# A GLA head's score matmuls issued in one burst, in turn over the array's column groups, and new lengths for fp32 matmuls in the planner

## The chip, the cores and the metric

One core of a Trainium2 chip. TensorE (PE) multiplies: it loads a stationary operand and streams the columns of a moving operand past it into PSUM. ScalarE (ACT) and VectorE (DVE) do element-wise work, GpSimd (POOL) a little, SyncE (SP) issues most DMAs. The metric is the device time of one execution in microseconds. Before the change it is 2159.78 us, the median of three runs (2157.18 to 2162.58).

## The reference

Two layers on 256 tokens of width 2048, everything in fp32. Layer 0 mixes tokens by native sparse attention (NSA), layer 1 by gated linear attention (GLA); each layer ends in a squared-ReLU MLP of width 8192. The part that matters here is the GLA mixer, 4 heads of key width 256 and value width 512:

```
h = rms_norm(x); q, k, v, g, r = split(h @ w_in)
log_a = log_sigmoid(g @ w_gate_up + b_gate) / 16
for each chunk of 64 tokens:
    cum   = cumsum(log_a)
    decay = exp(cum_i - cum_j) for j <= i
    att   = einsum(q_i, k_j, decay_ij)
    o     = (q * exp(cum)) @ state + att @ v
    state = exp(last) * state + (k * exp(last - cum)).T @ v
o = rms_norm(o) * silu(r);  x = x + o @ w_out
```

The kernel doesn't go chunk by chunk. For each head it makes the whole lower triangle of 256 x 256 scores with their decays, and multiplies it by the values.

## The kernel before, in words

The weights are fp32 and stream in by DMA. Each block of 128 x 1024 is split into a rounded part (ACT, the cast `wh`) and the rest (DVE, `wl`), and PE multiplies in three terms: high by high, high by low, low by high. These wide matmuls (`psa<-wh,op` and `psa<-wl,op`, 512 columns) fill nearly all of PE's time.

The mixers' own work is written as Python generators ("streams") that are stepped between the wide matmuls. The class `Plan` decides when: `mm` and the other helpers add an estimated cost to a clock for each engine (`W.run`), a stream yields the planned time from which its next piece is ready (`W.ready`) and the PSUM banks it needs (`{"aux": 1}`), and `W.tick`, called after every three wide matmuls, steps the streams whose time has come. So the order on each engine is fixed when the program is built, by the planner's costs. An fp32 matmul that isn't marked fp32r was counted as `max(4 * n / 2.4 + 3, 214)` ns (n moving columns).

The function `attn` (L1607 on) makes one head's scores. First the decays: products with the 0/1 matrix `cum`, exponentials on ACT, times keys and queries on DVE, into two tiles `e[0]` and `e[1]` (the head's 256 keys in two halves, `cc`; in the trace all these tiles are named `g`). Then the score matmuls by level: level 0 joins the two token blocks of 128, level 1 the halves of 64 within a block, level 2 those of 32, and levels 3 to 7 go down to single tokens. All are fp32, accumulated over `cc`:

- level 0: 2 matmuls, 128 stationary columns by 128 moving ones, into the bank `pc`;
- level 1: 4 of 64 by 64 and level 2: 8 of 32 by 32, into the bank `pa`, all of level 1 into partitions 0 to 63;
- levels 3 to 7: ten blocks (level, token block) of four matmuls, 32 by 64, into the bank `pq`; block i goes to partitions 32*(i%4), that is to one of the array's four groups of 32 columns.

The trace has every such fp32 matmul as two passes (two LDWEIGHTS and two MATMULs). In the old code the four matmuls of a block, eight passes, follow each other into the same column group:

```
for i, (l, t) in enumerate(blocks):
    for h in range(2):
        for cc in range(2):
            mm(pq[32 * (i % 4):32 * (i % 4) + 32, i // 4, own[h]], ...)
    if i % 4 == 3:
        yield 0.0
```

The yields part a head's 54 score matmuls into five bursts (2; 12; 16; 16; 8 matmuls) with three or six wide matmuls between them. Behind each bank ACT copies: `pc` and `pa` into `att` (one copy of 128 x 128, then six small ones), `pq` into the head of `e[0]`. Then PE transposes that (`psx<-cid,g`), DVE merges it into `att` with 20 predicated copies (L1715), ACT and DVE split `att` into `ath`, and `head_out` multiplies by the values (`psx<-g,ath`).

Of the kernel before, what the change touches and what calls it, by code (L numbers as in the profile page):

```python
# [18 lines left out]
P = 128  # L19
T = 256  # L20
NT = 2
# [102 lines left out]
def trunk_kernel(ctx: ExitStack, tc: tile.TileContext, a: dict, out: bass.AP):  # L124
# [3 lines left out]
    W = Plan()  # L128
    uid = [0]

    def nm(s):
        uid[0] += 1
        return f"{s}_{uid[0]}"
# [15 lines left out]
    def free(ap):  # L149
        n = 1  # L150
        for d in ap.shape[1:]:
            n *= d
        return n

    def in_psum(ap):
        return W.key(ap).startswith("ps")

    def mm(dst, lhsT, rhs, **kw):
        n = free(rhs)
        if lhsT.dtype == F32R:  # L160
            c = max(n / 2.4 + 13.0, 109.0)
        else:
            c = max(4 * n / 2.4 + 3, 214.0)
        W.run("pe", c, [dst], [lhsT, rhs])
        nc.tensor.matmul(dst, lhsT, rhs, skip_group_check=True, **kw)  # L165

# [27 lines left out]
    def copy(dst, src):  # L194
        W.run("act", free(src) * 0.833 + (60 if in_psum(src) else 100), [dst], [src])
        nc.scalar.copy(dst, src)  # L196

    def tt(dst, x, y, op):
        W.run("dve", free(dst) * 1.042 + 75, [dst], [x, y])
        nc.vector.tensor_tensor(dst, x, y, op=op)  # L200
# [46 lines left out]
    def aux(shape, dtype=F32):  # L247
        t = paux.tile(shape, dtype, tag="aux", name=nm("psx"))
        W.take("aux", t)
        return t  # L250
# [1229 lines left out]
    def gla(prep, after):  # L1480
        op = prep.op
        NLEV = 8
        with tc.tile_pool(name="gla1", bufs=1) as s1, tc.tile_pool(name="gla2", bufs=1) as s2:
# [131 lines left out]
            def attn(hd, kq, dg, wait, res):  # L1615


                while not all(w["done"] for w in wait):
                    yield 0.0
                e = []  # L1620
                for cc in range(2):
                    c = (2 * hd + cc) * P
                    yield W.ready(kq, cum, *las), {"g8": 1}
                    et = g8([P, NLEV, 2, P])
                    for t in range(NT):
                        yield 0.0, {"aux": 1}

                        pe_ = aux([P, 2, P])
                        for h in range(2):
                            mm(pe_.rearrange("p l k -> p (l k)"), las[2 * t + h][:, c:c + P],  # L1630
                               cum[:, 384 * h + t * P:384 * h + t * P + 2 * P], start=(h == 0), stop=(h == 1))
                        act(et[:, 0, t, :], pe_[:, t, :], AF.Exp)
                        act(et[:, 1, :, t * 64:t * 64 + 64], pe_[:, 1 - t, :].rearrange("p (s k) -> p s k", s=2), AF.Exp)
                        W.give(pe_, W.t["act"])
                        for b in (2 * t, 2 * t + 1):
                            yield 0.0, {"aux": 1}
                            pe_ = aux([P, NLEV - 2, 2, 32])
                            mm(pe_.rearrange("p l s k -> p (l s k)"), las[b][:, c:c + P], cum[:, 768:1152],
                               start=True, stop=True)
                            act(et[:, 2:NLEV, :, b * 32:b * 32 + 32], pe_, AF.Exp)  # L1640
                            W.give(pe_, W.t["act"])
                    for l in range(NLEV):
                        if l % 4 == 0:
                            yield W.ready(et)
                        hs = 128 >> l
                        ev = et[:, l, :, :].rearrange("p s (b r) -> p s b r", r=hs)
                        src = kq[:, cc, 0, :]
                        src = bass.AP(tensor=src.tensor, offset=src.offset,
                                      ap=[list(src.ap[0]), [T + hs, 2], [2 * hs, T // (2 * hs)], [1, hs]])
                        tt(ev, ev, src, ALU.mult)  # L1650
                    e.append(et)
                W.give(kq, W.t["dve"])
                att = s1.tile([P, 3, P], F32, name=nm("att")) if not shared else shared[0]
                if not shared:
                    shared.append(att)
                yield W.ready(*e), {"aux": 1}
                pc = aux([P, 512])
                for cc in range(2):
                    mm(pc[:, 0:P], e[cc][:, 0, 0, :], e[cc][:, 0, 1, :], start=(cc == 0), stop=(cc == 1))
                copy(att[:, 2, :], pc[:, 0:P])  # L1660
                W.give(pc, W.t["act"])
                own = [slice(64 * h, 64 * h + 64) for h in range(2)]
                yield 0.0, {"aux": 1}

                pa = aux([P, 512])
                for t in range(NT):
                    for cc in range(2):
                        tok = e[cc][:, 1, :, t * 64:t * 64 + 64]
                        mm(pa[0:64, t * P:t * P + 64], tok[:, 0, :], tok[:, 1, :], start=(cc == 0), stop=(cc == 1))
                    for h in range(2):  # L1670
                        for cc in range(2):
                            tok = e[cc][:, 2, :, t * 64 + 32 * h:t * 64 + 32 * h + 32]
                            mm(pa[64 * h:64 * h + 32, t * P + 64:t * P + 96], tok[:, 0, :], tok[:, 1, :],
                               start=(cc == 0), stop=(cc == 1))
                for t in range(NT):
                    ts(att[:, t, :], ident, dg[:, t:t + 1], None, ALU.mult)
                yield W.ready(pa)
                for t in range(NT):
                    copy(att[0:64, t, 64:128], pa[0:64, t * P:t * P + 64])
                    for h in range(2):  # L1680
                        copy(att[64 * h:64 * h + 32, t, 64 * h + 32:64 * h + 64],
                             pa[64 * h:64 * h + 32, t * P + 64:t * P + 96])
                give(pa)

                yield 0.0, {"aux": 1}
                pq = aux([P, 4, P])
                blocks = [(l, t) for l in range(3, NLEV) for t in range(NT)]
                for i, (l, t) in enumerate(blocks):
                    hs = 128 >> l
                    for h in range(2):  # L1690
                        for cc in range(2):
                            tok = e[cc][:, l, :, t * 64 + 32 * h:t * 64 + 32 * h + 32]
                            mm(pq[32 * (i % 4):32 * (i % 4) + 32, i // 4, own[h]], tok[:, 1, :],
                               tok.rearrange("p s (b r) -> p b s r", r=hs),
                               start=(cc == 0), stop=(cc == 1))
                    if i % 4 == 3:
                        yield 0.0
                W.give(e[1])
                at = e[0].rearrange("p l s k -> p (l s k)")[:, 0:3 * P].rearrange("p (i k) -> p i k", k=P)
                copy(at[:, 0:2, :], pq[:, 0:2, :])  # L1700
                copy(at[0:64, 2, :], pq[0:64, 2, :])
                W.give(pq, W.t["act"])
                yield W.ready(at), {"aux": 1}
                pl = aux([P, 512])
                for i in range(3):
                    n = P if i < 2 else 64
                    transpose(pl[:, i * P:i * P + n], at[0:n, i, :], ident[0:n, 0:n])
                W.give(e[0])
                yield W.ready(pl)
                for i, (l, t) in enumerate(blocks):  # L1710
                    hs = 128 >> l
                    for h in range(2):
                        dst = att[own[h], t, own[h]].rearrange("p (b s r) -> p b s r", s=2, r=hs)[:, :, 1, :]
                        W.run("dve", 110.0, [att], [pl])
                        nc.vector.copy_predicated(  # L1715
                            dst, lmask[own[h], l - 3, :].rearrange("p (b r) -> p b r", r=hs),
                            pl[own[h], 32 * i:32 * i + 32].rearrange("p (b r) -> p b r", r=hs))
                    if i % 4 == 3:
                        yield 0.0
                W.give(pl, W.t["dve"])  # L1720
                yield W.ready(att), {"ath": 1}
                ah = atile([P, 2, 3, P], F32R)
                copy(ah[:, 0, :, :], att)
                yield W.ready(ah)
                tt(ah[:, 1, :, :], att, ah[:, 0, :, :].bitcast(F32), ALU.subtract)
                res.append(ah)
# [261 lines left out]
```

## Time and profile before

| | before |
|---|---|
| median of three runs | 2159.78 us |
| the profiled execution's own time | 2158.59 us |
| its span, first to last instruction | 2156.8 us |
| PE busy | 2144.7 us, 99% |
| DVE busy | 1750.9 us, 81% |
| ACT busy | 1358.2 us, 63% |
| chain that ended last | PE 92%, DMA 5%, DVE 1%, ACT 1% |
| GLA's score matmuls in the trace | about 1170 to 1369 us, four heads |

"Busy" counts a matmul from its start to its modelled end. Since matmuls are pipelined, an engine can be 99% busy and still issue at very different rates; the time that one adds is read from the distance of starts.

### The profile page before, as it was taken

How to read it: one execution, taken by the hardware profiler on the slowest of the kernel's cores; microseconds unless marked ns; L12 is line 12 of the kernel's file. 1: busy time of each engine (PE TensorE's matmuls, PEld its weight loads, DVE VectorE, ACT ScalarE, POOL GpSimd, SP SyncE). 2: the span in 40 equal slices, each digit the busy share in tenths (PEclk: the TensorE clock that was granted, in tenths of full speed). 3: DMA queues.
4: the chain of work that ended last, by engine and by line, in shares of the span. 5: the costliest groups of instructions: out<-in, count | busy, mean ns of one | idle time of the engine just before them, and what ended most of it. 6: DMA issues, size and time to landing. Idle time of an engine off the chain costs nothing.

```text
span 2156.8 us, 29488 instructions
## 1 busy us (share of the span) xinstructions
PE 2144.7 (99%) x11019; PEld 1810.5 (84%) x11019; DVE 1750.9 (81%) x2382; ACT 1358.2 (63%) x2094; POOL 155.4 (7%) x189
## 2 busy tenths in 40 slices
PE   9999999999999999999999999999999999999999
PEld 7888888888888888888888888888888888888887
DVE  6778777789999999998666656667899999999985
ACT  6558676666666666666665555446666666666663
POOL 0010100000110011001100000000000010010010
PEclk9999999999999999999999999999999999999999
DMA  7553454769889879878655454456698798798784
GB/s 266 220 195 133 145 173 144 240 222 291 254 247 303 251 244 289 262 252 220 208 188 180 141 176 152 151 187 232 220 304 250 248 281 275 247 278 272 241 233 157
DMA packets 83167, 483.82 MB, mean 224 GB/s; under 512 B 10576, under 2 KB 13280, under 8 KB 35152
## 3 DMA queue, kind: packets, MB, share of 16 engines
q1 hardware_dynamic: 61344, 403.78, 51.3%
q0 software_dynamic: 21680, 78.15, 18.1%
q8 instruction: 87, 1.43, 0.2%
q14 instruction: 56, 0.46, 0.1%
HBM read 405.35 MB, written 2.10 MB: 189 GB/s over the span
## 4 chain that ended last, share of the span: by engine, by line
PE 92%; DMA 5%; DVE 1%; ACT 1%; issue 0%; SPq 0%; POOL 0%; POOLq 0%; DVEq 0%; ACTq 0%
PE psa L165 56%; PE psx L165 35%; DMA sraw<-sraw 3%; PE psx L169 2%; DMA sraw<-in_mlp_down_dram 1%; DMA raw<-in_nsa_in_dram 1%; ACT wh L196 1%; DVE wl L200 1%; DVE att L1715 0%; SPq L1829 0%; POOL sraw L337 0%; DVE kT L204 0%; DVE qT L200 0%; SPq L419 0%; SPq L411 0%
## 5 line engine op out<-in xcount | busy, mean ns | idle before, releaser
L165 PE MATMUL psa<-wh,op 128*128 128x512 f32 x2616 | 859.9, 393 | 2.0 <-ACT wh L196 2.0
L200 DVE TENSOR_TENSOR wl<-raw,wh 128x1024 fp32r<-128x1024 f32 (+1 forms) x529 | 642.2, 1219 | 219.8 <-ACT wh L196 217.9
L196 ACT CAST wh<-raw 128x1024 fp32r<-128x1024 f32 (+1 forms) x533 | 557.8, 1048 | 285.6 <-PE psa L165 239.5
L165 PEld LDWEIGHTS psa<-wh,op 128*128 128x128 f32 x2616 | 491.4, 188 | 104.8 <-ACT wh L196 2.8
L200 DVE TENSOR_TENSOR wl<-sraw,wh 128x1024 fp32r<-128x1024 f32 x392 | 473.4, 1219 | 62.5 <-ACT wh L196 59.5
L165 PE MATMUL psx<-op,wh 128*128 128x512 f32 (+1 forms) x2080 | 515.7, 390 | 0.0
L165 PE MATMUL psa<-wl,op 128*128 128x512 f32 x1308 | 511.5, 391 | 2.3 <-DVE wl L200 2.1
L196 ACT CAST wh<-sraw 128x1024 fp32r<-128x1024 f32 x392 | 410.1, 1052 | 152.8 <-PE psa L165 66.2
L165 PEld LDWEIGHTS psx<-op,wh 128*128 128x128 f32 (+1 forms) x2080 | 385.0, 188 | 78.1
L165 PE MATMUL psa<-wh,ht 128*128 128x512 f32 x1128 | 382.4, 392 | 0.8 <-ACT wh L196 0.5
L165 PEld LDWEIGHTS psx<-op,wl 128*128 128x128 f32 x2048 | 279.6, 190 | 19.9
L165 PEld LDWEIGHTS psa<-wl,op 128*128 128x128 f32 x1308 | 245.9, 188 | 50.7 <-DVE wl L200 5.5
L165 PE MATMUL psx<-op,wl 128*128 128x256 f32 x2048 | 286.0, 282 | 0.0
L165 PEld LDWEIGHTS psa<-wh,ht 128*128 128x128 f32 x1128 | 212.7, 189 | 41.0 <-issue 1.1
L165 PE MATMUL psa<-wl,ht 128*128 128x512 f32 x564 | 221.8, 393 | 0.6 <-DVE wl L200 0.6
L337 POOL DMA_DIRECT2D sraw<-sraw x140 | 120.2, 955 | 1294.2 <-DVE pz L200 429.3
L204 DVE SCALAR_TENSOR_TENSOR xt<-psa,r,xt 128x512 f32<-128x512 f32 x212 | 157.2, 744 | 17.5 <-PE psa L165 16.7
L196 ACT COPY zz<-psx 128x256 f32<-128x256 f32 x128 | 47.5, 371 | 149.4 <-PE psx L165 149.1
L165 PEld LDWEIGHTS psa<-wl,ht 128*128 128x128 f32 x564 | 106.7, 189 | 16.7 <-DVE wl L200 1.8
L200 DVE TENSOR_TENSOR sraw<-sraw,sraw 128x1024 f32<-128x1024 f32 x84 | 102.5, 1221 | 1.0
L200 DVE TENSOR_TENSOR zz<-psx,zz 128x256 f32<-128x256 f32 x128 | 53.6, 419 | 14.2 <-ACT zz L196 14.2
L196 ACT CAST ht<-pz 128x896 fp32r<-128x896 f32 (+1 forms) x40 | 37.1, 928 | 28.8 <-DVE pz L204 27.8
(195 smaller groups left out, 1191.4 us busy)
## 6 DMA issues: line engine op xcount, KB each, us to landing
raw<-in_mlp_up_dram SPq DMA_DIRECT2D x128, 1024.0 KB, 7.5
sraw<-in_mlp_down_dram SPq DMA_DIRECT2D x112, 1024.0 KB, 11.3
sraw<-sraw POOLq DMA_DIRECT2D x140, 512.0 KB, 9.3
raw<-in_gla_in_dram SPq DMA_DIRECT2D x48, 1024.0 KB, 4.8
raw<-in_nsa_in_dram SPq DMA_DIRECT2D x38, 1024.0 KB, 4.9
raw<-in_nsa_out_dram SPq DMA_DIRECT2D x16, 1024.0 KB, 4.8
raw<-in_mlp_down_dram SPq DMA_DIRECT2D x16, 1024.0 KB, 4.9
raw<-in_gla_out_dram SPq DMA_DIRECT2D x16, 1024.0 KB, 4.8
```

The costliest lines, as they stand in the source:

```text
L165: nc.tensor.matmul(dst, lhsT, rhs, skip_group_check=True, **kw)
L169: nc.tensor.transpose(dst, src, idn)
L196: nc.scalar.copy(dst, src)
L200: nc.vector.tensor_tensor(dst, x, y, op=op)
L204: nc.vector.scalar_tensor_tensor(dst, x, s, y, op0=op0, op1=op1)
L337: nc.gpsimd.dma_start(dst, src, accum_op=ALU.add)
```

## The change

It does three things. In `mm` an fp32 matmul is planned at 109 ns or a little more if its stationary operand has over 64 columns, otherwise at the number of those columns plus 2 ns. In `attn` the 54 score matmuls are issued in one step, with two PSUM banks asked for at once. And their order changes: level 1 of the second token block now goes to partitions 64 to 127, levels 1 and 2 alternate between two column groups, and levels 3 to 7 go round the four column groups, one matmul each, instead of finishing a block first. The copies, transposes and predicated copies stay the same in number.

```diff
         else:
-            c = max(4 * n / 2.4 + 3, 214.0)
+
+            c = max(n / 2.4 + 13.0, 109.0) if free(lhsT) > 64 else free(lhsT) + 2.0
...
-                yield W.ready(*e), {"aux": 1}
-                pc = aux([P, 512])
+                yield W.ready(*e), {"aux": 2}
+
+                pa = aux([P, 512])
                 for cc in range(2):
-                    mm(pc[:, 0:P], e[cc][:, 0, 0, :], e[cc][:, 0, 1, :], start=(cc == 0), stop=(cc == 1))
-                copy(att[:, 2, :], pc[:, 0:P])
-                W.give(pc, W.t["act"])
-                own = [slice(64 * h, 64 * h + 64) for h in range(2)]
-                yield 0.0, {"aux": 1}
-
-                pa = aux([P, 512])
+                    mm(pa[:, 2 * P:3 * P], e[cc][:, 0, 0, :], e[cc][:, 0, 1, :], start=(cc == 0), stop=(cc == 1))
+                for cc in range(2):
+                    for t in range(NT):
+                        tok = e[cc][:, 1, :, t * 64:t * 64 + 64]
+                        mm(pa[64 * t:64 * t + 64, t * P:t * P + 64], tok[:, 0, :], tok[:, 1, :], start=(cc == 0), stop=(cc == 1))
                 for t in range(NT):
                     for cc in range(2):
-                        tok = e[cc][:, 1, :, t * 64:t * 64 + 64]
-                        mm(pa[0:64, t * P:t * P + 64], tok[:, 0, :], tok[:, 1, :], start=(cc == 0), stop=(cc == 1))
-                    for h in range(2):
-                        for cc in range(2):
+                        for h in range(2):
                             tok = e[cc][:, 2, :, t * 64 + 32 * h:t * 64 + 32 * h + 32]
                             mm(pa[64 * h:64 * h + 32, t * P + 64:t * P + 96], tok[:, 0, :], tok[:, 1, :],
                                start=(cc == 0), stop=(cc == 1))
+                pq = aux([P, 4, P])
+                blocks = [(l, t) for l in range(3, NLEV) for t in range(NT)]
+                for i0 in range(0, len(blocks), 4):
+                    for h in range(2):
+                        for cc in range(2):
+                            for i in range(i0, min(i0 + 4, len(blocks))):
+                                l, t = blocks[i]
+                                tok = e[cc][:, l, :, t * 64 + 32 * h:t * 64 + 32 * h + 32]
+                                mm(pq[32 * (i % 4):32 * (i % 4) + 32, i // 4, own[h]], tok[:, 1, :],
+                                   tok.rearrange("p s (b r) -> p b s r", r=128 >> l),
+                                   start=(cc == 0), stop=(cc == 1))
...
                 yield W.ready(pa)
-                for t in range(NT):
-                    copy(att[0:64, t, 64:128], pa[0:64, t * P:t * P + 64])
+                copy(att[:, 2, :], pa[:, 2 * P:3 * P])
+                for t in range(NT):
+                    copy(att[0:64, t, 64:128], pa[64 * t:64 * t + 64, t * P:t * P + 64])
...
-                yield 0.0, {"aux": 1}
-                pq = aux([P, 4, P])
-                blocks = [(l, t) for l in range(3, NLEV) for t in range(NT)]
-                for i, (l, t) in enumerate(blocks):
...
-                    if i % 4 == 3:
-                        yield 0.0
                 W.give(e[1])
+                yield W.ready(pq)
```

What this does to the order is shown at three places. The first is PE at the first GLA head, before: `psx_10816` is the bank `pc`, `psx_10823` is `pa`, `psx_10854` is `pq`, the two `g` tiles are `e[0]` and `e[1]`, and the `psa` rows are wide matmuls.

```order
L165 MATMUL psx_10816<-g_1928_10629 128x128
L165 MATMUL psx_10816<-g_1943_10712 128x128
L165 MATMUL psa_10800<-wh_10713,op_9725 128x512
L165 MATMUL psa_10800<-wl_10714,op_9725 128x512
L165 MATMUL psa_10800<-wh_10713,op_9725 128x512
L165 MATMUL psx_10823<-g_1928_10629 64x64
L165 MATMUL psx_10823<-g_1943_10712 64x64
L165 MATMUL psx_10823<-g_1928_10629 32x32
L165 MATMUL psx_10823<-g_1943_10712 32x32
```

The same place on PE after the change, where `psx_10816` is `pa` and `psx_10831` is `pq`:

```order
L166 MATMUL psx_10816<-g_1928_10629 128x128
L166 MATMUL psx_10816<-g_1943_10712 128x128
L166 MATMUL psx_10816<-g_1928_10629 64x64 x2
L166 MATMUL psx_10816<-g_1943_10712 64x64 x2
L166 MATMUL psx_10816<-g_1928_10629 32x32 x2
L166 MATMUL psx_10816<-g_1943_10712 32x32 x2
L166 MATMUL psx_10816<-g_1928_10629 32x32 x2
L166 MATMUL psx_10816<-g_1943_10712 32x32 x2
L166 MATMUL psx_10831<-g_1928_10629 32x64 x4
L166 MATMUL psx_10831<-g_1943_10712 32x64 x4
L166 MATMUL psx_10831<-g_1928_10629 32x64 x4
```

The burst starts behind the same wide matmul as before and now holds all 54 matmuls; the 15 wide ones that stood between the bursts and the 3 to 6 behind them stand behind it. From the burst's end to the transposes of the `pq` copy there are 15, 12, 18 and 21 wide matmuls in the four heads; before there were 6 behind the last burst in every head.

The second place is ACT behind that burst, before, where `psx_10816`, `psx_10823` and `psx_10854` are the three banks and `wh` the casts of weights:

```order
L196 COPY att_10790<-psx_10816 128x128
L196 CAST wh_10838<-raw_10700 128x1024
L196 COPY att_10790<-psx_10823 64x64
L196 COPY att_10790<-psx_10823 32x32 x2
L196 COPY att_10790<-psx_10823 64x64
L196 COPY att_10790<-psx_10823 32x32 x2
L196 COPY g_1928_10629<-psx_10854 128x256
L196 COPY g_1928_10629<-psx_10854 64x128
L196 CAST wh_10903<-raw_10700 128x1024
```

And ACT at the same place after:

```order
L197 COPY att_10790<-psx_10816 128x128
L197 COPY att_10790<-psx_10816 64x64
L197 COPY att_10790<-psx_10816 32x32 x2
L197 COPY att_10790<-psx_10816 64x64
L197 COPY att_10790<-psx_10816 32x32 x2
L197 CAST wh_10884<-raw_10700 128x1024
L197 COPY g_1928_10629<-psx_10831 128x256
L197 COPY g_1928_10629<-psx_10831 64x128
```

The cast of weights that stood between the first copy and the six small ones now stands between these and the copies of `pq`. In the second and third head no cast stands there, in the fourth two activations of the values and one cast.

The third place is DVE in NSA, some 120 us into the program, where the new lengths move a compression's work. Before (`kT` are compressed keys, `qT` the operand of the next compression, `t` and `pe` its sources):

```order
L200 TENSOR_TENSOR kk<-rca_1171,rcb_1172 64x32
L204 SCALAR_TENSOR_TENSOR kT_138<-psx_1196,gcol,kT_138 128x16
L204 SCALAR_TENSOR_TENSOR kT_139<-psx_1196,gcol,kT_139 128x16
L204 SCALAR_TENSOR_TENSOR kT_140<-psx_1196,gcol,kT_140 128x16
L204 SCALAR_TENSOR_TENSOR kT_141<-psx_1196,gcol,kT_141 128x16
L200 TENSOR_TENSOR qT_1206<-t_141_894,pe 128x4x8x15
L204 SCALAR_TENSOR_TENSOR kT_138<-psx_1181,gcol,kT_138 128x2x128
```

DVE there after:

```order
L201 TENSOR_TENSOR kk<-rca_1185,rcb_1186 64x32
L201 TENSOR_TENSOR qT_1196<-t_141_894,pe 128x4x8x15
L205 SCALAR_TENSOR_TENSOR kT_138<-psx_1174,gcol,kT_138 128x2x128
L205 SCALAR_TENSOR_TENSOR kT_139<-psx_1174,gcol,kT_139 128x2x128
L205 SCALAR_TENSOR_TENSOR kT_138<-psx_1209,gcol,kT_138 128x16
L205 SCALAR_TENSOR_TENSOR kT_139<-psx_1209,gcol,kT_139 128x16
L205 SCALAR_TENSOR_TENSOR kT_140<-psx_1209,gcol,kT_140 128x16
```

The sum for `qT` now stands ahead of the four narrow `kT` steps. Besides this place and the GLA stage, where some streams' pieces shift by three to six wide matmuls, the order on PE, ACT and DVE is as before, and on POOL and SP nothing moves.

## Rows read from the trace of the kernel before

**Rows 1.** The page: busy time by engine, PE's granted clock, one costly group.
```profile
PE 2144.7 (99%) x11019; PEld 1810.5 (84%) x11019; DVE 1750.9 (81%) x2382; ACT 1358.2 (63%) x2094; POOL 155.4 (7%) x189
...
PEclk9999999999999999999999999999999999999999
...
L196 ACT CAST wh<-raw 128x1024 fp32r<-128x1024 f32 (+1 forms) x533 | 557.8, 1048 | 285.6 <-PE psa L165 239.5
```

**Rows 2.** Waits of PE: us in total, times, longest.
```profile
PE psa L165 <- DVE wl L200: 2.8, 7, 0.8
...
PE psx L165 <- DVE qT L200: 0.8, 1, 0.8
```

**Rows 3.** Timeline of PE, first head: start us, length us, what, count.
```profile
1171.12 0.39 PE L165 MATMUL psa<-wh,op 128*128 128x512 f32 x1
1171.44 1.33 PE L165 MATMUL psx<-g 128*64 128x64 f32 x24
1172.70 0.50 PE L165 MATMUL psa<-wh,op 128*128 128x512 f32 x1
1173.03 0.39 PE L165 MATMUL psa<-wl,op 128*128 128x512 f32 x1
...
1173.96 0.40 PE L165 MATMUL psa<-wh,op 128*128 128x512 f32 x1
1174.29 1.40 PE L165 MATMUL psx<-g 128*32 128x64 f32 x32
...
1175.95 0.39 PE L165 MATMUL psa<-wl,op 128*128 128x512 f32 x1
1176.18 0.40 PE L165 MATMUL psa<-wh,op 128*128 128x512 f32 x1
...
1178.40 0.40 PE L165 MATMUL psa<-wh,op 128*128 128x512 f32 x1
1178.73 1.04 PE L165 MATMUL psx<-g 128*32 128x64 f32 x16
1179.70 0.50 PE L165 MATMUL psa<-wh,op 128*128 128x512 f32 x1
1180.03 0.39 PE L165 MATMUL psa<-wl,op 128*128 128x512 f32 x1
```

**Rows 4.** The same, cut off inside the warm-up and three bursts.
```profile
4.90 0.60 PE L165 MATMUL psx<-idle 128*128 128x256 f32 x2
...
4.90 0.81 PE L165 MATMUL psx<-idle 128*128 128x256 f32 x3
...
1171.44 0.62 PE L165 MATMUL psx<-g 128*64 128x64 f32 x7
...
1171.44 0.70 PE L165 MATMUL psx<-g 128*64 128x64 f32 x12
...
1174.29 0.41 PE L165 MATMUL psx<-g 128*32 128x64 f32 x4
...
1174.29 1.17 PE L165 MATMUL psx<-g 128*32 128x64 f32 x28
...
1178.73 0.76 PE L165 MATMUL psx<-g 128*32 128x64 f32 x12
```

**Rows 5.** Groups of PE by form: count, busy us, mean ns of one.
```profile
L165 PE MATMUL psx<-g 128*32 128x64 f32 x320 | 15.3, 224 | 0.0
```

**Rows 6.** Timeline of ACT, first head.
```profile
1172.85 0.95 ACT L196 COPY att<-psx 64x64 f32<-64x64 f32 x6 [0.26 <-PE psx L165]
...
1179.81 0.53 ACT L196 COPY g<-psx 128x256 f32<-128x256 f32 x2 [6.01 <-PE psx L165]
```

**Rows 7.** Timeline of ACT and PE in NSA.
```profile
120.60 0.27 ACT L192 ACTIVATE kT<-psx,gcol 128x16 fp32r<-128x16 f32 x1 [0.76 <-PE psx L169]
...
128.43 0.74 PE L165 MATMUL psx<-op,qT 128*128 128x256 f32 x4 [0.82 <-DVE qT L200]
```

**Rows 8.** Stretch table at the end: length, busy us by engine (count), clock, DMA.
```profile
2154.00:2157.00 3.00, 0.00 (x0) 0.00 (x0) 0.00 (x0) 0.00 (x0) 0.00 (x0) 0.67 0.23 87
```

More of the change, by code (lines that the diff above doesn't have):

```diff
@@ L1674, in attn @@
                                start=(cc == 0), stop=(cc == 1))
+                own = [slice(64 * h, 64 * h + 64) for h in range(2)]
+                pq = aux([P, 4, P])
[9 more added lines that the diff above has]
+                                   start=(cc == 0), stop=(cc == 1))
                 for t in range(NT):
@@ L1683, in attn @@
                 give(pa)
-                yield 0.0, {"aux": 1}
-                pq = aux([P, 4, P])
-                blocks = [(l, t) for l in range(3, NLEV) for t in range(NT)]
-                for i, (l, t) in enumerate(blocks):
[L1689 to L1695, printed above, removed]
-                    if i % 4 == 3:
-                        yield 0.0
                 W.give(e[1])
+                yield W.ready(pq)
                 at = e[0].rearrange("p l s k -> p (l s k)")[:, 0:3 * P].rearrange("p (i k) -> p i k", k=P)
```

## The prediction, made before the changed kernel ran

> **What bounds the kernel now.** I read the page's first two parts first: PE is busy 99% of the span, and its granted clock is 0.9 or more of 2.4 GHz in all 40 slices [rows 1]. Then the waits of PE: the largest entry sums to 2.8 us and the only one in NSA's compression to 0.8 us [rows 2]. So the kernel is as long as PE's queue, and what counts is the distance from one start to the next. For that I read the timeline of PE at the first GLA head [rows 3]: two wide matmuls that follow each other start 0.23 us apart (1175.95 and 1176.18), and what a burst of score matmuls costs is the time from the start of the wide matmul before it to that of the second one behind it, less two such steps.
>
> - levels 1 and 2: 1171.12 to 1173.03, 1.91 - 0.46 = 1.45 us
> - levels 3 and 4: 1173.96 to 1175.95, 1.53 us; the burst of levels 5 and 6 that follows repeats this
> - level 7: 1178.40 to 1180.03, 1.17 us
>
> With the second burst of 32 passes that is 5.68 us for a head. Level 0's four passes stand behind a wide matmul in both versions and are left out of both sums. The other three heads have the same bursts (320 passes of 32 by 64 in all, 80 for each head [rows 5]).
>
> **What a pass costs.** In the warm-up a pass of an fp32 matmul with 256 columns takes 0.81 - 0.60 = 0.21 us, 0.82 ns a column (three end so much after two [rows 4]). For 64 columns that makes 53 ns, and the first four passes of a block, alone in their column group, do come some 60 ns apart ((0.41 - 0.22)/3, where 0.22 is the length of one [rows 4, 5]). So a pass alone is bound by its own column stream. But further into the same burst 24 passes take 1.17 - 0.41 = 0.76 us, 32 ns each [rows 4]: there the next block has started in another column group while the first is still at work. Two streams do run beside each other. In level 2, with 32 columns, five passes take 0.70 - 0.62 = 0.08 us, 16 ns each [rows 4]; PE can start passes at least that fast. In level 7 the last four of 16, alone again, come (1.04 - 0.76)/4 = 70 ns apart [rows 3, 4]; in pairs that makes 35.
>
> **The change part by part.** Going round the four column groups lets four streams run side by side. By 56/4 a pass (between the 53 and the 60) would cost 14 ns; nothing in the trace shows starts faster than 16 ns, nor more than two groups at work. Between 14 and 32 ns I take 16, the fastest row. For one head:
>
> - from the shape of 128 stationary columns into that of 64: 0.09 us, as before (1171.44 against 1171.12 + 0.23)
> - level 1: eight passes, two groups side by side: 0.05 us for the slow first one and four rounds of 0.06, 0.30 us. One after another it would be 0.53
> - from 64 columns to 32: two rounds of levels 1 and 2 took 1.26 us (1171.44 to 1172.70), 0.63 each, of which level 1 is 0.05 + 4 x 0.06 = 0.29 and level 2 eight passes of 16 ns, 0.13; that leaves some 0.22 for two changes of shape. Now there is one, 0.11 us
> - level 2: 16 passes of 16 ns, 0.26 us
> - levels 3 to 6: 64 passes of 16 ns, 1.02 us
> - level 7: only two groups have work, 16 passes of 35 ns, 0.56 us
> - back to wide matmuls: the last pass of level 7 starts at 1178.73 + 1.04 - 0.23 = 1179.54, the next wide one at 1179.70, the one behind it 0.33 later instead of 0.23: 0.16 + 0.10 - 0.04 = 0.22 us
>
> Together 2.56 us against 5.68. A head gains 3.12 us, four heads 12.5 us. With 14 ns it would be 13.0; with pairs only (32 ns) levels 3 to 6 cost 2.05 and four heads gain 8.4.
>
> *A rule that speaks against it.* The row above has two column groups overlap at 32 ns where one alone takes some 60. The Trainium skill, "TensorE: Matmul & The Clock Gate", section "The mechanism", says that loading weights overlaps running matmuls only when they use different row groups. All passes here use all rows, so by that rule nothing would overlap and the head would cost what the second rival below has; the trace contradicts it for two groups, and no row shows four.
>
> The copies behind the burst stay seven and two. `pa` is finished before `pq`'s first matmul, so its seven copies (six of them 0.95 us [rows 6]) run on ACT beside the second half of the burst. What is queued behind them: in the first head a cast of weights of 1.05 us [rows 1], which waits for the first three wide matmuls behind the burst (0.7 us), and then the two copies of `pq`, 0.53 us [rows 6]. PE's transposes, who wait for these, stand 15 wide matmuls behind the burst, 3.45 us; the chain needs 0.7 + 1.05 + 0.53 and some 0.3 between, 2.6 us. In the second head there are only 12, 2.8 us, but no cast. So the wait is covered; without the cover it would cost up to a cast, 1 us, in a head. That casts and weights pause for a burst costs nothing, as ACT and DVE have time left (63% and 81% busy [rows 1]).
>
> The planner's new lengths also move NSA's compression. There PE waits 0.82 us for `qT` from DVE [rows 7]. DVE's sum for `qT` now stands ahead of four narrow steps that alternate with ACT, and ACT gets a cast to do in the 0.76 us that it sat idle before the first of these [rows 7]. It can gain the whole wait or, where ACT's cast holds the narrow steps, lose some 0.7 us; I take a gain of 0.4.
>
> The sum is 12.5 + 0.4 = 12.9 us on the profiled execution's 2158.6 us (span 2156.8 and 1.8 around it): 2145.7. The median of the runs shown lies 1.2 us above that execution, so the forecast is **2147 us**, 0.6% faster.
>
> **The rivals.**
>
> *Only pairs of groups overlap*, or starts have a floor above 16 ns. For it: the trace never shows more than two groups, each with a queue of its own weights and results. Against it: nothing that is shared runs out at two, and level 2 starts at 16 ns. With 32 ns four heads gain 8.4 + 0.4: 2151 us. *A page's floor.* The 16 ns starts of level 2 stand against a figure of the Trainium skill, same page, section "Wait — 56ns, not 53.3ns?": starts never come closer than about 25 ns. By it, an estimate, the time would be 2150 us; the trace has starts closer than that between column groups.
>
> *The order gains nothing, or serializes.* If a change of column group had to wait for the pass before it, passes would cost their own stream: level 1 0.53, level 2 16 x 27 ns = 0.43, levels 3 to 6 64 x 56 ns = 3.58, level 7 16 x 70 ns = 1.12, with 0.42 for changes of shape 6.08 us, 0.4 more than before: 2161 us. If overlap stayed as it was, with 1.18 us for 32 passes (1.40 - 0.22 [rows 3]), a head would cost 0.09 + 0.30 + 0.11 + 0.26 + 2 x 1.18 + 0.81 + 0.22 = 4.15 and four gain 6.1 by the bursts' merging alone: 2153 us.
>
> *The clock falls.* A burst keeps PE for some 3 us on strips of 32 columns, where before 1.4 us was the longest. If the granted clock fell to the 1.2 GHz level there, the burst would take 2.6 us more, and every wide matmul until it rises 0.46 instead of 0.23 us. The gain of 3.1 us a head is gone when the low clock lasts two wide matmuls beyond the burst; from ten on the kernel is slower by over 0.3%, and with 15 it is at 2159.8 - 0.4 + 4 x (2.6 + 3.45 - 3.1) = 2171 us. Against it: the clock stays at 0.9 or more through five bursts a head, and the only stretch that shows it down is the last 3 us, after PE had stopped [rows 8].
>
> *The planner moves more than meant.* The order is the same outside the two places, so this is worth under 1 us either way.
>
> **How the numbers follow.** Forecast, with 14 to 20 ns a pass: 0.68, its own range 2144.5 to 2150. Pairs or a floor, 2150 to 2152.5: 0.17. Merging alone, 2152.5 to 2156: 0.08. Serialized, about 2161: 0.03. The clock, about 2171: 0.02. Faster than all of these, by waits that I have not seen: 0.02. The range from 2143.5 to 2154.5 leaves out the last cases and half of merging, and holds a run-to-run spread of 2 us on top. A measurement of this kernel tells from no change what is over about 0.3%, 6.5 us: faster means below 2153.3. That is the forecast, the pairs, the surprise and a little of merging, 0.88; within 0.3% is the rest of merging and most of serializing, 0.09; slower is the clock and the remainder, 0.03.
>
> **What would show it.** In the profile after, one row of 108 passes a head, some 3 us from the wide matmul before to the second behind, less 0.46. Right: 32 passes of levels 3 and 4 start within 0.5 us, and the page's row of 320 passes falls from 15.3 us busy to about a half. Pairs: 1 us for them. Serialized: 1.8 us. The transposes `psx<-cid,g` show no wait for ACT, and the wait for `qT` in NSA shrinks. The prediction is wrong if the granted clock shows a gap in the GLA stage, or if new waits for `att` or `g` stand among PE's.

## The result and the profile after

The changed kernel takes 2143.68 us, the median of six runs (2142.58 to 2144.95), beside 2159.51 for the kernel before in the same comparison: a ratio of 0.9929 with a 95% interval of 0.9918 to 0.994. In two later comparisons it was 0.9938 (0.9925 to 0.9951) and 0.9933 (0.9919 to 0.9947). So it is 13 to 16 us faster; 12.9 were forecast.

The page first: busy time by engine, and PE's granted clock (the rows that answer to [rows 1]).

```profile
span 2143.2 us, 29481 instructions
...
PE 2131.0 (99%) x11019; PEld 1802.2 (84%) x11019; DVE 1750.5 (82%) x2382; ACT 1359.7 (63%) x2094; POOL 155.5 (7%) x189
...
PEclk9999999999999999999999999999999999999999
```

PE is as full as before, with the same 11019 matmuls in 13.6 us less. A digit of the clock's row is the mean of some 54 us and would hide a dip of 3 us, so here is the stretch around the first burst by itself (length, busy us by engine and count, granted clock, DMA share, GB/s):

```profile
1170.00:1175.00 5.00, 5.00 (x119) 4.31 (x118) 2.87 (x6) 2.23 (x9) 0.00 (x0) 1.00 0.31 88
```

The granted clock is 1.00, the 2.4 GHz level, and the stretches around the other three bursts show the same. The timeline of PE at the first head (start, length, what, count) answers to [rows 3]:

```profile
1170.82 0.40 PE L166 MATMUL psa<-wh,op 128*128 128x512 f32 x1
1171.05 2.81 PE L166 MATMUL psx<-g 128*128 128x128 f32 x108
1173.79 0.50 PE L166 MATMUL psa<-wh,op 128*128 128x512 f32 x1
1174.13 0.40 PE L166 MATMUL psa<-wl,op 128*128 128x512 f32 x1
...
1177.09 0.39 PE L166 MATMUL psa<-wh,op 128*128 128x512 f32 x1
1177.32 0.58 PE L170 MATMUL psx<-cid,g 128*128 128x128 f32 x3
...
1178.17 0.40 PE L166 MATMUL psa<-wl,op 128*128 128x512 f32 x1
```

One row of 108 passes is the whole head (a merged row carries the shape of its first pass). From 1170.82 to 1174.13 less two wide steps of 0.23 it costs 2.85 us, of which level 0 is 0.45. Before, the same 108 passes cost 6.14 (0.45 for level 0 and 5.69 for levels 1 to 7, whose rounded parts add up to 5.68), so a head gains 3.29 us and four gain 13.2; the other three heads have 2.85 too. Cut off inside the burst, the same view shows the rate (it answers to [rows 4]):

```profile
1171.05 1.42 PE L166 MATMUL psx<-g 128*128 128x128 f32 x31
...
1171.05 1.45 PE L166 MATMUL psx<-g 128*128 128x128 f32 x34
...
1171.05 1.90 PE L166 MATMUL psx<-g 128*128 128x128 f32 x66
...
1171.05 2.25 PE L166 MATMUL psx<-g 128*128 128x128 f32 x91
```

From the 34th pass to the 66th it takes 0.45 us, 14 ns a pass: a quarter of the 56 that one column group needs. (The first block's passes start 56 ns apart in the trace before, at 1174.37, 1174.42, 1174.48 and 1174.53; in the trace after, the passes of each group still do, and four such rows lie side by side.) By groups of form (it answers to [rows 5]) the 320 passes are busy for 6.7 us in place of 15.3:

```profile
L166 PE MATMUL psx<-g 128*32 128x64 f32 x320 | 6.7, 222 | 0.0
```

The mean length of one hardly changed, 222 ns for 224; what changed is how many lie beside each other. ACT at the same head (it answers to [rows 6]):

```profile
1172.49 1.27 ACT L197 COPY att<-psx 128x128 f32<-128x128 f32 x7 [1.66 <-PE psx L166]
1174.83 1.05 ACT L197 CAST wh<-raw 128x1024 fp32r<-128x1024 f32 x1 [1.07 <-issue]
1175.91 0.53 ACT L197 COPY g<-psx 128x256 f32<-128x256 f32 x2
```

The seven copies run beside the second half of the burst and end with it. The two copies behind the cast end at 1176.44, 0.9 us before PE's transposes at 1177.32, which wait for nothing. NSA's compression on PE (it answers to [rows 7]), first the wide matmul ahead of it before, then the two rows after, and all waits of PE after:

```profile
127.22 0.39 PE L165 MATMUL psa<-wh,op 128*128 128x512 f32 x1
```

```profile
126.66 0.39 PE L166 MATMUL psa<-wh,op 128*128 128x512 f32 x1
126.93 0.74 PE L166 MATMUL psx<-op,qT 128*128 128x256 f32 x4
```

```profile
PE psa L166 <- DVE wl L201: 3.2, 7, 0.8
PE psa L166 <- ACT wh L197: 3.1, 7, 1.3
PE psx L166 <- DVE idle L291: 1.2, 1, 1.2
PE psx L166 <- DVE ath L201: 0.3, 1, 0.3
```

The wait for `qT` is gone: the step from the wide matmul to `psx<-op,qT`, 1.21 us before (of which the 0.23 of a wide matmul isn't a wait), is 0.27. That is 0.9 to 1.0 us. The waits for weights are 6.3 us where the profile before had 5.3; 3.6 of the 6.3 fall into the first 60 us and the rest into the first layer's MLP. The last of the experiments show that this sum varies from run to run.

How much of the time belongs to GLA can be read from the starts of the same wide matmuls: the one ahead of the first score matmuls, and the 997th (`psa`, 512 columns) behind it, which comes after the fourth head. Before (with the wide matmul behind level 0, from which its 0.45 us is read: 0.91 - 0.46):

```profile
1169.97 0.40 PE L165 MATMUL psa<-wh,op 128*128 128x512 f32 x1
...
1170.88 0.40 PE L165 MATMUL psa<-wl,op 128*128 128x512 f32 x1
...
1445.76 0.39 PE L165 MATMUL psa<-wh,op 128*128 128x512 f32 x1
```

After, where the first of the two is the row at 1170.82 above:

```profile
1433.10 0.39 PE L166 MATMUL psa<-wh,op 128*128 128x512 f32 x1
```

This GLA stretch takes 275.79 us before and 262.28 after, 13.5 less, of which the bursts are 13.2. In the three other traces with the changed kernel's `attn` it takes 262.29 to 262.32. The rest of the span is less steady: 1877.0 to 1884.5 us in the twelve traces of all kernels here, 1881.0 before and 1880.9 after.

### The profile page after: what moved, and what is told of

The parts are those of the page before. It is cut to its first block, busy times and chain, and to the rows that moved or that the text cites. A ratio compares the mean times of both kernels' runs of the same rounds, so it can differ in the third digit from the quotient of the medians.

```text
span 2143.2 us, 29481 instructions
## 1 busy us (share of the span) xinstructions
PE 2131.0 (99%) x11019; PEld 1802.2 (84%) x11019; DVE 1750.5 (82%) x2382; ACT 1359.7 (63%) x2094; POOL 155.5 (7%) x189
## 4 chain that ended last, share of the span: by engine, by line
PE 93%; DMA 5%; DVE 1%; ACT 1%; issue 0%; SPq 0%; POOL 0%; POOLq 0%; DVEq 0%; ACTq 0%
PE psa L166 56%; PE psx L166 34%; DMA sraw<-sraw 3%; PE psx L170 2%; DMA sraw<-in_mlp_down_dram 2%; ACT wh L197 1%; DVE wl L201 1%; DMA xs<-in_x_dram 0%; DVE att L1714 0%; DMA raw<-in_nsa_in_dram 0%; POOL sraw L338 0%; ACT op L193 0%; SPq L1828 0%; SPq L420 0%; DVE op L205 0%
## 5 line engine op out<-in xcount | busy, mean ns | idle before, releaser
L205 DVE SCALAR_TENSOR_TENSOR xt<-psa,r,xt 128x512 f32<-128x512 f32 x212 | 156.9, 743 | 15.8 <-PE psa L166 15.1
L201 DVE TENSOR_TENSOR zz<-psx,zz 128x256 f32<-128x256 f32 x128 | 53.4, 417 | 14.2 <-ACT zz L197 14.1
```

What stands on the lines that cost most here:

```text
L205: nc.vector.scalar_tensor_tensor(dst, x, s, y, op0=op0, op1=op1)
```

## The experiments

The first four ran beside the same runs of before (median 2158.7 us), the next four likewise (2158.7), the last two beside 2159.66.

**The planner's lengths alone.** The one line in `mm`, on the kernel before.

> The kernel before with only the planner's new lengths for fp32 matmuls; the bursts of score matmuls stay five a head, block after block. Theory (the gain is the bursts' cost, plus one wait in NSA): each head's bursts still cost 6.14 us with level 0 (0.45 + 1.45 + 1.53 + 1.53 + 1.17), the wait of 0.82 us for qT near 127 us is gone, and the time is 0.5 to 1 us under before, near 2158.5. Rival (the new lengths let the planner place the whole GLA stage better, which is where the part of the gain beyond 12.9 us comes from): 2 to 4 us faster, near 2156.5.

Measured: 2158.07 us, ratio 1.0 (0.9991 to 1.0009). The bursts cost 6.14 us a head, as before, the GLA stretch takes 275.82 us (275.79 before), and the wait for `qT` is gone:

```profile
127.91 0.39 PE L165 MATMUL psa<-wh,op 128*128 128x512 f32 x1
128.20 0.74 PE L165 MATMUL psx<-op,qT 128*128 128x256 f32 x4
```

The theory holds; the rival's 2 to 4 us are just outside the interval, and GLA did not change. One microsecond is less than these runs can tell as time, so for that size the trace is the measurement.

**The bursts with the old lengths.** The changed kernel with `c = max(4 * n / 2.4 + 3, 214.0)` put back.

> The changed kernel with the planner's old length for fp32 matmuls. Theory (bursts): one burst of 2.85 us a head with level 0, as in the changed kernel, so 4 x 3.3 = 13.2 us under before, near 2146; the wait of 0.82 us for qT in NSA is back. Rival (planner): only some 11 to 12 us under before, with new waits of PE behind the bursts, since the planner takes a burst for 11.6 us.

Measured: 2145.89 us, ratio 0.9942 (0.9931 to 0.9954). Each burst costs 2.85 us, and PE's waits have NSA's again:

```profile
PE psx L166 <- DVE qT L201: 0.8, 1, 0.8
```

No wait behind the bursts appears: the number of wide matmuls between burst and transposes is 15, 12, 18 and 21 with either length. The GLA stretch takes 262.31 us, so the new lengths do nothing there.

**One burst, old order in it.**

```diff
-                            for i in range(i0, min(i0 + 4, len(blocks))):
+                    for i in range(i0, min(i0 + 4, len(blocks))):
+                        for h in range(2):
+                            for cc in range(2):
```

(and levels 1 and 2 as before, level 1 in partitions 0 to 63).

> One burst a head and the new lengths, but in it the old order: level 1 into partitions 0 to 63, and levels 3 to 7 block after block, so that only neighbouring blocks overlap. Theory (most of the gain is four column groups side by side, 14 ns a pass): the burst costs 5.05 us (0.45 + 0.09 + 1.22 + 2 x 1.18 + 0.81 + 0.12), so 4 x 1.1 = 4.4 us and up to 1 us from NSA's wait, near 2154.5. Rival (most of the gain is that PE changes shape less often): near 2149.

Measured: 2152.47 us, ratio 0.9973 (0.9964 to 0.9982).

```profile
1169.61 0.40 PE L166 MATMUL psa<-wh,op 128*128 128x512 f32 x1
1169.84 4.75 PE L166 MATMUL psx<-g 128*128 128x128 f32 x108
1174.52 0.50 PE L166 MATMUL psa<-wh,op 128*128 128x512 f32 x1
1174.86 0.39 PE L166 MATMUL psa<-wl,op 128*128 128x512 f32 x1
```

5.25 - 0.46 = 4.79 us a head, 5.05 expected; I had left out that blocks 4 and 8 overlap with the ones ahead of them too once no wide matmul stands between. Merging alone is worth 4 x 1.35 = 5.4 us, with NSA's wait 6.4; measured 6.2. That lies between the two prices, nearer the theory's: merging is less than half of the gain, but more than the 4.4 us that I gave it.

**The changed kernel again,** beside its parts.

> The changed kernel once more, beside the same runs of before as its parts. Theory (bursts 13.2 us, NSA's wait 0.8 to 1): 14 us under before, 2144 to 2146; of the 15.8 us of the first comparison 1 to 2 are then spread between runs. Rival (a third part of the gain, outside bursts and wait): again 15.5 to 16 us.

Measured: 2145.44 us, ratio 0.9938 (0.9925 to 0.9951): 13.3 us. It is the theory's; the 15.8 us of the first comparison lay above it.

**Five bursts, in turn over the groups.** The kernel before with only this in levels 3 to 7:

```diff
-                for i, (l, t) in enumerate(blocks):
+                for i0 in range(0, len(blocks), 4):
                     for h in range(2):
                         for cc in range(2):
+                            for i in range(i0, min(i0 + 4, len(blocks))):
```

> The kernel before (five bursts a head, old planner's lengths, level 1 in partitions 0 to 63), with only the order inside the bursts of levels 3 to 7 changed to one matmul for each column group in turn. Theory (four groups side by side): the two bursts of 32 passes fall from 1.53 to some 0.85 us, the one of 16 from 1.17 to 0.92, so 1.6 us a head, 6.4 in all: near 2152.3. Rival (changes of shape are what costs): the bursts change by less than 0.2 us each, under 2 us in all.

Measured: 2151.69 us, ratio 0.9967 (0.9955 to 0.9979).

```profile
1176.26 0.40 PE L165 MATMUL psa<-wh,op 128*128 128x512 f32 x1
1176.59 0.65 PE L165 MATMUL psx<-g 128*32 128x64 f32 x32
1177.17 0.50 PE L165 MATMUL psa<-wh,op 128*128 128x512 f32 x1
1177.51 0.39 PE L165 MATMUL psa<-wl,op 128*128 128x512 f32 x1
```

The burst of 32 costs 1.25 - 0.46 = 0.79 us against 1.53; the one of 16 falls to 0.88. A head gains 1.77 us, four gain 7.1: the measured 7.0. The order of levels 3 to 7 alone and the merging alone add up to 12.5 us, and the changed kernel brings 13.2. It also has levels 1 and 2 in a new order, which no run tests alone: from the first of their passes to the last it is 1.13 us in the merged burst above and 0.63 in the changed kernel, four times 0.5 us. So the three parts add up to more than the whole; they share some of the gain.

**Two groups at a time.** `range(0, len(blocks), 2)` and `min(i0 + 2, ...)` in the changed kernel.

> The changed kernel with levels 3 to 6 issued for two blocks at a time, so that matmuls alternate between two column groups instead of four. Theory (each group is bound by its own stream of 56 ns a pass, and groups run side by side): 28 ns a pass, the burst 2.85 + 64 x 0.014 = 3.7 us, a little less where the next pair starts early; 3 us longer in all. Rival (what the alternation buys is that weights load ahead, and two groups do for that): still about 14 to 16 ns a pass, the burst 2.85 to 2.95 us.

Measured (a single run): 2148.62 us; what counts is the trace, cut off inside the burst and whole.

```profile
1170.88 1.53 PE L166 MATMUL psx<-g 128*128 128x128 f32 x34
...
1170.88 2.08 PE L166 MATMUL psx<-g 128*128 128x128 f32 x66
...
1170.88 2.96 PE L166 MATMUL psx<-g 128*128 128x128 f32 x108
```

32 passes take 0.55 us, 17 ns each, and the burst costs 3.01 us. This is nearly the rival's number, and my theory's 28 ns is wrong as a rate for this order. But the rival's reason (weights that load ahead) does not follow either, since a group's own passes start 56 ns apart here as in the changed kernel. The rows of before have eight passes of one group every (1.17 - 0.41)/3 = 0.25 us [rows 4], though eight times 56 ns is 0.45: the next block starts when three passes of the running one are still to come. With pairs, 16 passes should then come every 0.25 us, 16 ns each, which is what the burst shows. PE starts other groups' passes while a few of a group still wait; with two at a time that reaches into the next pair. The trace shows it, since a pass's record has its operand's pattern and so its level: the first pass of level 5 starts at 1172.58, the last of level 4 at 1172.74, and pairs follow each other every 0.26 us. So four groups are at work for 0.16 of each 0.26 us.

**One group after the other.** The accumulation of a strip's blocks is interleaved in this kernel, which changes the scores; only its time is read.

```diff
-                for i0 in range(0, len(blocks), 4):
+                for g in range(4):
...
-                            for i in range(i0, min(i0 + 4, len(blocks))):
+                            for i in range(g, len(blocks), 4):
```

> The changed kernel with levels 3 to 7 issued one column group after the other: 24, 24, 16 and 16 passes in a row into the same strip. Theory (a pass alone takes its own stream): 56 ns a pass and 70 in level 7, less some overlap of three or four passes where the group changes: 2 x (16 x 56 + 8 x 70) + 2 x 16 x 56 = 4.7 us less 0.6 for levels 3 to 7 instead of 1.46, the burst 5.3 to 5.6 us, 10 to 11 us longer in all than the changed kernel, near 2155. Rival (merging the bursts brought the gain, the order little): the burst 3.0 to 3.5 us.

Measured (a single run): 2155.59 us.

```profile
1167.98 0.40 PE L166 MATMUL psa<-wh,op 128*128 128x512 f32 x1
1168.22 5.40 PE L166 MATMUL psx<-g 128*128 128x128 f32 x108
...
1173.88 0.39 PE L166 MATMUL psa<-wl,op 128*128 128x512 f32 x1
```

5.90 - 0.46 = 5.44 us, as the theory has it. The same 108 passes in one burst cost 2.85, 3.01, 4.79 or 5.44 us, by their order (and, for 4.79, by the partitions of level 1).

**Carried on.** The last levels under the same two rules: level 1 in strips of 32 columns, level 7 over four groups.

```diff
-                        mm(pa[64 * t:64 * t + 64, t * P:t * P + 64], tok[:, 0, :], tok[:, 1, :], ...)
+                        for s in range(2):
+                            r0 = 64 * t + 32 * s
+                            mm(pa[r0:r0 + 32, t * P:t * P + 64], tok[:, 0, 32 * s:32 * s + 32], tok[:, 1, :], ...)
...
+                            r0 = 64 * h + 32 * t
+                            mm(pq[r0:r0 + 32, 2, own[h]], tok[:, 1, :], ...)
...
-                    n = P if i < 2 else 64
-                    transpose(pl[:, i * P:i * P + n], at[0:n, i, :], ident[0:n, 0:n])
+                    transpose(pl[:, i * P:(i + 1) * P], at[:, i, :], ident)
```

> The changed kernel carried on: level 1 as strips of 32 columns too (8 matmuls of 32 by 64 in four groups, so that PE changes shape once less), and level 7 spread over all four groups instead of two, its results in other partitions, which makes the third transpose a full one of 128 rows. Theory (streams per group and changes of shape): level 1 falls from 0.38 us with the change of shape to 0.25, level 7 from 0.56 to 0.28, the transposes by 0.3, together 0.7 us a head, 2.8 in all: near 2141.5. Rival (four streams already fill what the groups share: level 7's strided reads don't run faster over four groups): level 7 stays at 0.5 us or more, 1.5 us in all, not to be told from the changed kernel.

Measured: 2141.21 us, ratio 0.9918 (0.9904 to 0.9931).

```profile
1167.62 0.40 PE L166 MATMUL psa<-wh,op 128*128 128x512 f32 x1
1167.86 2.40 PE L166 MATMUL psx<-g 128*128 128x128 f32 x116
1170.18 0.50 PE L166 MATMUL psa<-wh,op 128*128 128x512 f32 x1
1170.52 0.40 PE L166 MATMUL psa<-wl,op 128*128 128x512 f32 x1
...
1173.49 0.39 PE L166 MATMUL psa<-wh,op 128*128 128x512 f32 x1
1173.72 0.49 PE L170 MATMUL psx<-cid,g 128*128 128x128 f32 x3
1173.97 0.49 PE L166 MATMUL psa<-wh,op 128*128 128x512 f32 x1
1174.29 0.39 PE L166 MATMUL psa<-wl,op 128*128 128x512 f32 x1
```

The burst costs 2.44 us instead of 2.85, with eight passes more. The step over the transposes, 1173.49 to 1174.29, is 0.80 us instead of 1.08. That is 0.69 us a head, 2.8 in all, as expected. Once more, beside the changed kernel:

> The carried-on kernel a second time, on the same chip and beside the same runs of before as the changed kernel. Its trace has 2.44 us for a burst instead of 2.85 and 0.28 us less around the transposes: theory 2.7 us a run under the changed kernel. Rival (PE's time comes back as waits for weights in the MLPs, whose sum varies by 2 to 3 us from run to run anyway): no difference.

> The changed kernel beside it: 13.2 us of bursts and 1.0 us of NSA's wait under before, so a ratio of 0.9934; with the carried-on kernel at 0.9922 (theory) or the same (rival).

Measured: 2142.36 us, ratio 0.9914 (0.99 to 0.9928), beside 2145.29 us, 0.9933 (0.9919 to 0.9947). The medians differ by 2.9 us but the intervals overlap: by time alone it is not settled. In GLA it is: the stretch takes 259.81 us in both traces of the carried-on kernel, 2.5 us less than in any of the changed kernel. The rest of the span hides this: in the last two profiles it is 1883.3 us for the carried-on kernel and 1877.0 for the changed one, so that the span is longer with it, 2143.1 us against 2139.3. Waits for weights are a part of that (why the rest varies beyond them is not shown). These waits are the first two rows here, of the changed kernel's last profile and of the carried-on one's:

```profile
PE psa L166 <- DVE wl L201: 2.1, 4, 0.8
...
PE psa L166 <- ACT wh L197: 0.9, 2, 0.7
```

```profile
PE psa L166 <- DVE wl L201: 3.2, 7, 0.8
PE psa L166 <- ACT wh L197: 1.8, 5, 1.1
```

The changed kernel has 3.0 us here and 6.3 in its first profile: 3 us between two executions of one program.

## Why the prediction was right, step by step

- *What bounds the kernel.* Right: 13.2 us less work on PE's queue became 13 to 16 us.
- *16 ns a pass in levels 3 to 6.* 14 were measured. I had stopped at the fastest row of before; a quarter of a single group's 56 ns was the better figure. The bound of 14 ns was in the prediction. The 16 ns of level 2 was no floor but two groups at 31 ns each (32 columns), and "nothing in the trace shows starts faster than 16 ns" was a wrong reading: the trace before has starts of neighbouring blocks some 5 ns apart, at 1174.534 and 1174.539.
- *The head.* 2.56 us forecast without level 0, 2.40 measured: by the starts in the trace some 0.10 of the difference lies in levels 3 to 6, the rest in levels 1 and 2.
- *The copies behind the burst.* Right to 0.1 us: 0.85 us of cover counted (3.45 against 2.6), 0.9 found.
- *NSA's wait.* 0.4 taken between -0.7 and +0.8, 0.9 to 1.0 measured. This step was mis-sized: the row's 0.82 us leaves out a part of the gap (the wide matmul ahead still counts as running), and with DVE's sum moved up the whole gap went.
- *The sum.* 12.9 forecast; by the traces 13.2 + 1.0 = 14.2, or 14.5 with the whole GLA stretch. Measured 15.8, 13.3 and 14.4. The first comparison's extra is within the 7 us or so by which the rest of the span varies. So 2147 us was 3.3 too long for that comparison: some 1.6 are the terms above, the rest is how the runs fell. The result of 2143.68 lies below the forecast's own range (from 2144.5) and only 0.2 us inside the wider one (from 2143.5); the later medians, 2145.44 and 2145.29, lie inside both.
- *Rivals.* Pairs of groups only: fell, four run. Merging alone: the kernel that comes nearest gains 5.4 us from the bursts; the rival's 6.1 had levels 1 and 2 in the new order, which that kernel leaves out. Serialized: with one group after the other the passes do follow each other at 56 ns, and the burst costs 5.44 us; in turn over the groups they do not. The clock: 1.00 around all four bursts. The planner: nothing outside NSA.
- *The two rules of the Trainium skill* ("TensorE: Matmul & The Clock Gate"). That weights load beside running matmuls only where row groups differ (section "The mechanism") is contradicted: all passes use all rows, and four column groups work side by side at 14 ns a pass, with weight loads of 110 ns beside them. The floor of some 25 ns between starts (section "Wait — 56ns, not 53.3ns?") does not hold across column groups: passes 32 to 34 above add 0.03 us together, and the mean is 14.

## What to carry to other kernels

Small fp32 matmuls into separate 32-column groups ran beside each other, each group at the pace of its own stream (56 ns a pass of 64 columns, 14 ns over four groups); so put consecutive matmuls into different groups, and spread the work evenly over all four. Keep matmuls of one shape together, since changes of shape cost too: among wide matmuls a burst of 32 passes cost 0.79 us, though 32 x 14 ns are 0.45. Look for this where PE is busy all the time: a busy share says nothing of the rate, and the distance of starts does.

## What the runs showed of the hardware that was not expected

PE starts the passes of different column groups out of program order: with blocks of eight passes, the next group starts when three of the last one's are still to come, a period of 0.25 us in place of 0.45. In the trace before, where levels 3 and 4 can be told apart by their operands' patterns, a pass of level 4 starts at 1174.793 and the last three of level 3 at 1174.842, 1174.899 and 1174.954. That is why two groups at a time got 17 ns and not 28. And level 7's strided operand, 70 ns a pass in one group, speeds up over four groups as the others do: its 16 passes start within 0.52 us in the changed kernel and within 0.27 in the carried-on one, whose burst is 0.41 us shorter.
